# Down projection of sixteen feed-forward blocks with seven products instead of eight per pair of token tiles

## The chip, the cores and the metric

The kernel runs on one core of one Trainium2 chip. The metric is the device time of one execution in microseconds (us). The kernel before took 1143.12, 1145.43 and 1145.72 us in three runs, a median of 1145.43 us.

## The reference, cut to what matters

One layer works on 512 latent tokens and 128 context tokens of width 1024: modulation, a normalised projection, an RWKV-7 branch and a neighbourhood-attention branch, an output projection, and last a gated feed-forward network. Only the last is touched here:

```python
FF_HIDDEN = -(-8 * D_MODEL // (3 * 256)) * 256          # 2816 = 22 blocks of 128
x = x + g1 * (merged @ p["w_out"])
h2 = _rmsnorm(x, p["norm2_g"]) * (1.0 + sc2) + sh2
x = x + g2 * ((jax.nn.silu(h2 @ p["ffn_w1"]) * (h2 @ p["ffn_w3"])) @ p["ffn_w2"])
```

`g2` is a gate over the 1024 columns, one row for the latent tokens and one for the context tokens. Everything is float32.

## The kernel before, in words

The 640 tokens are five tiles of 128; tiles 0 to 3 are latent, tile 4 is context. TensorE multiplies in a rounded float32 format, so every operand is split in two: a rounded part `hi` (a cast on ScalarE) and the remainder `lo` (a subtraction on VectorE). A product is three matmuls: hi by hi, lo by hi, hi by lo. For weights, the names are `wst` (as loaded), `whi` and `wlo`.

**Up projection.** The 2816 hidden features are 22 blocks of 128. Blocks 0 and 1 are computed the plain way (`conv_gen`, beside the tail of the stage before). Each block from 2 on is computed by `pair(ft, ...)`: seven products, each of 4 x 3 matmuls of 128x128 by 128x320, into three accumulators `A_`, `B_`, `C_` (Winograd's form of Strassen's method over two halves of the width and two halves of the tokens, and the weight sums `ws` are made by `w_sum`). After each of the seven products the table `PRM["wt"]` (for block 2: `PRM["wf"]`) says which steps the other engines get next. A bare letter belongs to the block in hand, `<` to the block before it (its tail: `x h m i o`, which end in the hidden block `u` and its split), `-` to this block's own weights, `>` to the weights of the next block (`s1` to `s4` sums, `ha la hb lb` the casts of the first two of its four weight tiles).

**Down projection.** After the blocks of a part (0 to 5, 6 to 11, 12 to 17, 18 to 21; `fp=(6, 12, 18)`) `down_gen` multiplies them by their rows of `ffn_w2`, 512 columns at a time (`n` is 0 or 1): for each half, each hidden block and each of five token tiles, three matmuls of 128x128 by 128x512. `w2c(n, f)` is a tile of `ffn_w2` for the blocks f and f+1, side by side, 512 columns each. `add_gated` takes a finished accumulator, multiplies it by the gate `G` and adds it to `x2[i]`, the layer's running result; in the last part the rows are then stored.

**What sets the order.** TensorE, VectorE, ScalarE and GpSimd (POOL) work in program order here (`manual_schedule`). SyncE (SP) issues the loads; a scheduler puts them in order, and SP too works in order: a load whose buffer is not free holds back those behind it. Weight buffers come in two pools, which `weights(...)` opens. Home 0 has two buffers for `wst`, home 1 has one; each has two for `whi` and two for `wlo`. `w_stage` loads the `ffn_w1` tile ("g") of a block into home 1, and the `ffn_w3` tile ("u") into home 0. The raw tile in home 1 can be overwritten only when the last reader of the one before it is done.

Of the kernel before, what the change touches and what calls it, by code (L numbers as in the profile page):

```python
# [22 lines left out]
XB, WAB, FA = 4, 8, 2  # L23
# [35 lines left out]
     "120:W2S3A4R3W3S4X3R4X4 186:T3U3H3J3 198:T4U4H4J4 206:K0D1M0D3D2P2D4K1K2Q2V0K3N0 222:K5K7K6K8M2P3K4Q3V2N2"),  # L59
# [4 lines left out]
        ">s3 V1 N1 g >s1",  # L64
        "z >s2 >ha M3",
        "v V3 N3 >s4 >la",
        "w >hb >lb",
# [3 lines left out]
        "u -ld <i <o",  # L71
        ">s3 g >s1",
        "z >s2 >ha",
# [3 lines left out]
    fp=(6, 12, 18), h2e="dpddddpddd", x0e="a", ze="aa", y2=1, y1=0, sc=3, sr=3, sp=1, mg=1.915, h1=0.952,  # L77
# [37 lines left out]
def body(ctx: ExitStack, tc: tile.TileContext, xs, xp, cols, consts, w_ada, b_row, w_rw, w_qkv,  # L115
# [112 lines left out]
    def drain(g):  # L228
        for _ in g:
            pass  # L230
# [1505 lines left out]
    x2 = [xpool.tile([P, 1024], F32, name=f"x2_{i}") for i in range(5)]  # L1736
    G = xpool.tile([P, 2, 1024], F32, name="G")
# [5 lines left out]
    def load_gate(b):  # L1743
        ad = adr[:, :]
        for g in range(2):
            sp.dma_start(G[:, g, :], bass.AP(ad.tensor, ad.offset + g * 6144 + b * 512, [[0, P], [1, 1024]]))

    def add_gated(ps, i, n, c, a=0, b=512):
        g, sl = 0 if i < 4 else 1, slice(n * 512 + a, n * 512 + b)
        tt = sb.tile([P, 512], F32, tag="tt", bufs=2, name=nm("tt"))[:, a:b]  # L1750
        dve.scalar_tensor_tensor(out=tt, in0=ps[:, a:b], scalar=c, in1=G[:, g, sl], op0=ALU.mult, op1=ALU.mult)  # L1751
        dve.tensor_tensor(out=x2[i][:, sl], in0=x2[i][:, sl], in1=tt, op=ALU.add)
# [97 lines left out]
    steps = dict(D=t_sum, P=t_hi, Q=t_lo, M=lambda i: conv_mul(i), V=lambda i: conv_hi(i), N=lambda i: conv_lo(i), K=lambda i: first_prep(i), A=n_add, S=n_square, R=n_rstd, X=n_scale, T=lambda i: n_out(i, 0), U=lambda i: n_out(i, 1), H=lambda i: n_split(i, 0), J=lambda i: n_split(i, 1),  # L1850
# [21 lines left out]
    load_gate(10)  # L1872
    u = {}

    def hidden(ft):
        u[ft] = qp.tile([P, 2, NT], F32R, tag="q", bufs=6, name=nm("u"))
# [23 lines left out]
    def conv_a(i):  # L1900
        ca[i] = sb.tile([P, NT], F32, tag="a", bufs=2, name=nm("a"))[:, :H2]

    def conv_u(i):
        ft, n = i // 2, i % 2
        if n == 0 and ft not in u:
            hidden(ft)
        return [u[ft][:, p_, H2 * n:H2 * n + H2] for p_ in range(2)]

    def conv_mul(i):
        if i not in ca:  # L1910
            conv_a(i)
        p1, p3 = cps.pop(i)
        act.activation(ca[i], p1[:, :H2], AF.Silu)
        dve.tensor_tensor(out=ca[i], in0=ca[i], in1=p3[:, :H2], op=ALU.mult)

    def conv_hi(i):
        act.copy(conv_u(i)[0], ca[i])

    def conv_lo(i):
        hi, lo = conv_u(i)  # L1920
        dve.tensor_tensor(out=lo, in0=ca[i], in1=hi.bitcast(F32), op=ALU.subtract)
# [38 lines left out]
    def pair(ft, tag, old, now, nxt):  # L1960
# [4 lines left out]
        p1, u2, u3 = [sb.tile([P, H2], F32, tag=t, bufs=1, name=nm(t)) for t in ("p1", "u2", "u3")]  # L1965
# [10 lines left out]
        out = dict(p=lambda: act.copy(p1, A_), u=lambda: add(u2, B_, p1),  # L1976
                   g=lambda: act.activation(a[:, :H2], A_, AF.Silu),
                   z=lambda: add(u3, B_, p1), v=lambda: add(c2[:, H2:], C_, u3), w=lambda: add(c2[:, :H2], B_, p1),
                   x=lambda: add(u2, C_, u2), h=lambda: act.activation(a[:, H2:], u2, AF.Silu), m=mul, i=lambda: act.copy(u[ft][:, 0, :], a),
                   o=lambda: eng_x(PRM["oe"]).tensor_tensor(out=u[ft][:, 1, :], in0=a, in1=u[ft][:, 0, :].bitcast(F32),  # L1980
                                                            op=ALU.subtract))
        x = B2
        prods = ((A_, "a", 0, x[0, 0], True), (B_, "b", 0, BT[2], True), (A_, "a", 512, x[1, 0], False),
                 (B_, "b", 512, BT[3], False), (C_, "c", 0, BT[1], True), (B_, "d", 0, BT[4], False),
                 (C_, "c", 512, x[1, 1], False))
        for j, (ps, k, o_, x_, st) in enumerate(prods):
            for _ in mm4(ps, w[k], o_, x_, first=st, more=not st):
                pass
            for e in PRM["wf" if ft == FA else "wt"][j].split():
                if e in at1:  # L1990
                    at1[e]()
                    continue
                d = {"<": old, "-": now, ">": nxt}.get(e[0], out)
                f = d.pop(e.strip("<->"), None)
                if f:
                    f()
        return out

    at1 = {f"{k}{i}": lambda k=k, i=i: steps[k](i) for k in "PQMVN" for i in range(5)}
# [34 lines left out]

    fts = [list(range(a, b)) for a, b in zip((0,) + PRM["fp"], PRM["fp"] + (NFT,))]
    with tc.manual_schedule(engines=FIRST):
# [3 lines left out]
        for i in (1, 3):  # L2040
            conv_a(i)
        for part, fs in enumerate(fts):
            old, first, todo = {}, [], [f for f in fs if f >= FA]
            for j, ft in enumerate(todo):
                if ft < fs[-1]:
                    w_stage(ft + 1)
                    nxt = preps(ft + 1)
                else:
# [5 lines left out]
                old, now = pair(ft, ("acc", "tp")[j % 2], old, now, nxt), nxt  # L2054
            run(old, "x h m i o")
            for n in range(2):
                fin = part == len(fts) - 1 and n == 1
                pss = {}
                drain(down_gen(pss, fs, n, fin, first))
                if n == 0:  # L2060
                    first = [wload(w2c(1, f)) for f in fs[0:2 * PRM["pf"]:2]]
                elif not fin:
                    w_stage(fs[-1] + 1)
                    now = preps(fs[-1] + 1)
                    run(now, PRM["w0"])
                for i, t in pss.items():
                    down_out(i, t, n, fin, part)
# [112 lines left out]
```

## Time and profile before

| | before |
|---|---|
| median of three runs | 1145.43 us (1143.12 to 1145.72) |
| span of the profiled execution | 1142.3 us |
| what the runs show around that span | 0.8 to 3.4 us (the three times less 1142.3) |
| TensorE busy | 1108.0 us, 97% of the span |
| VectorE, ScalarE, POOL busy | 777.2, 537.9, 195.8 us |
| first block computed by `pair` starts | 741.2 us |
| one block of `pair`, steady | 12.32 us |
| one part's down projection with six blocks | 40.78 us |

The profile gives one execution: busy times of the engines, groups of instructions by line with their mean duration, what ended each wait, and the order in time. Matmuls overlap, so the pace of TensorE is read from the distance of starts and not from a duration. Times below without a unit of their own are in us from the start of the span.

### The profile page before, as it was taken

How to read it: one execution, taken by the hardware profiler on the slowest of the kernel's cores; microseconds unless marked ns; L12 is line 12 of the kernel's file. 1: busy time of each engine (PE TensorE's matmuls, PEld its weight loads, DVE VectorE, ACT ScalarE, POOL GpSimd, SP SyncE). 2: the span in 40 equal slices, each digit the busy share in tenths (PEclk: the TensorE clock that was granted, in tenths of full speed). 3: DMA queues.
4: the chain of work that ended last, by engine and by line, in shares of the span. 5: the costliest groups of instructions: out<-in, count | busy, mean ns of one | idle time of the engine just before them, and what ended most of it. 6: DMA issues, size and time to landing. Idle time of an engine off the chain costs nothing.

```text
span 1142.3 us, 26868 instructions
## 1 busy us (share of the span) xinstructions
PE 1108.0 (97%) x11160; PEld 980.2 (86%) x11160; DVE 777.2 (68%) x1641; ACT 537.9 (47%) x1060; POOL 195.8 (17%) x262
## 2 busy tenths in 40 slices
PE   5999999999999999999899999999999999999998
PEld 4688878789888988888898788999899989998997
DVE  4565465669658847945787846996478647874775
ACT  4444566665565665567343525654134413441340
POOL 1163244330101212110100511210101010101000
PEclk8999999999999999999999999999999999999999
DMA  9753677654423433344734962223212321232122
GB/s 340 262 107 102 187 268 259 200 151 112 126 64 98 130 104 94 107 108 107 266 92 126 264 214 72 78 89 112 72 56 93 111 74 56 93 106 80 56 93 93
DMA packets 60482, 149.16 MB, mean 131 GB/s; under 512 B 7460, under 2 KB 22436, under 8 KB 60360
## 3 DMA queue, kind: packets, MB, share of 16 engines
q1 hardware_dynamic: 54312, 129.85, 34.8%
q0 software_dynamic: 4032, 14.68, 6.5%
q10 hardware_dynamic: 2016, 2.90, 0.8%
q8 instruction: 88, 1.44, 0.5%
q14 instruction: 34, 0.28, 0.1%
HBM read 118.41 MB, written 14.32 MB: 116 GB/s over the span
## 4 chain that ended last, share of the span: by engine, by line
PE 76%; DVE 8%; issue 7%; ACT 4%; DMA 3%; POOL 1%; SPq 0%; ACTq 0%; DVEq 0%; POOLq 0%
PE acc L311 23%; PE f L1883 23%; PE fl L223 10%; PE mm L223 5%; DMA wa<-in_w_ada_dram 3%; PE psa L1044 1%; DVE RL L1330 1%; DVE pr L1326 1%; PE lg L959 1%; PE pt L988 1%; PE po L1006 1%; DMA win<-in_rpbp_dram 1%; PE w L1446 1%; PE fl L587 1%; PE w L1189 1%
## 5 line engine op out<-in xcount | busy, mean ns | idle before, releaser
L1883 PE MATMUL f<-t,whi 128*128 128x320 f32 x640 | 141.7, 310 | 0.2
L311 PE MATMUL acc<-whi,u 128*128 128x512 f32 (+1 forms) x448 | 136.1, 386 | 0.0
L1883 PE MATMUL f<-b,whi 128*128 128x320 f32 x608 | 135.0, 310 | 0.4 <-DVE b L212 0.4
L223 PE MATMUL fl<-h,whi 128*128 128x320 f32 x672 | 120.9, 320 | 0.0
L1883 PEld LDWEIGHTS f<-t,whi 128*128 128x128 f32 x640 | 106.8, 188 | 0.8 <-issue 0.4
L223 PEld LDWEIGHTS fl<-h,whi 128*128 128x128 f32 x672 | 101.2, 188 | 4.8 <-issue 0.2
L192 ACT CAST whi<-wst 128x1024 fp32r<-128x1024 f32 (+1 forms) x77 | 79.3, 1033 | 53.4 <-PE acc L311 41.6
L1883 PEld LDWEIGHTS f<-b,whi 128*128 128x128 f32 x608 | 101.8, 188 | 1.1 <-issue 0.6
L1883 PE MATMUL f<-t,wlo 128*128 128x320 f32 x320 | 98.9, 309 | 0.0
L311 PEld LDWEIGHTS acc<-whi,u 128*128 128x128 f32 x448 | 83.5, 188 | 16.6
L1883 PE MATMUL f<-b,wlo 128*128 128x320 f32 x304 | 94.1, 309 | 0.0
L1936 ACT CAST whi<-ws 128x1024 fp32r<-128x1024 f32 x40 | 42.0, 1051 | 104.4 <-PE f L1883 45.6
L1950 POOL TENSOR_TENSOR ws<-wst 128x512 f32<-128x512 f32 x20 | 29.2, 1462 | 334.6 <-DVE wlo L1939 226.3
L311 PE MATMUL acc<-wlo,u 128*128 128x512 f32 (+1 forms) x224 | 86.3, 385 | 0.0
L311 PE MATMUL acc<-whi,h 128*128 128x512 f32 x240 | 79.2, 404 | 0.8 <-DVE h L436 0.8
L195 DVE TENSOR_TENSOR wlo<-wst,whi 128x1024 fp32r<-128x1024 f32 (+2 forms) x57 | 60.2, 1066 | 27.8 <-ACT whi L192 27.2
L1751 DVE SCALAR_TENSOR_TENSOR tt<-acc,G 128x512 f32<-128x512 f32 (+1 forms) x51 | 34.7, 680 | 59.6 <-PE acc L311 44.7
L223 PE MATMUL fl<-h,wlo 128*128 128x320 f32 x336 | 62.7, 318 | 0.0
L1936 ACT CAST whi<-wst 128x1024 fp32r<-128x1024 f32 (+1 forms) x48 | 41.3, 869 | 42.3 <-PE acc L311 37.6
L1883 PEld LDWEIGHTS f<-t,wlo 128*128 128x128 f32 x320 | 60.1, 188 | 0.0
L1939 DVE TENSOR_TENSOR wlo<-ws,whi 128x1024 fp32r<-128x1024 f32 x40 | 55.5, 1387 | 5.4 <-ACT whi L1936 5.4
L191 POOL DMA_DIRECT2D wlo<-wst x28 | 24.8, 886 | 191.4 <-ACT wlo L190 169.9
(341 smaller groups left out, 2534.0 us busy)
## 6 DMA issues: line engine op xcount, KB each, us to landing
wst<-in_w_dram SPq DMA_DIRECT2D x66, 512.0 KB
wst<-in_w_rw_dram SPq DMA_DIRECT2D x31, 512.0 KB
wlo<-wst POOLq DMA_DIRECT2D x28, 512.0 KB, 4.7
wa<-in_w_ada_dram SPq DMA_DIRECT2D x24, 512.0 KB
f<-in_w_ada_dram SPq DMA_DIRECT2D x16, 512.0 KB
wst<-in_w_qkv_dram SPq DMA_DIRECT2D x12, 512.0 KB
o<-o_d SPq DMA_DIRECT2D x14, 320.0 KB
x<-in_xs_dram SPq DMA_DIRECT2D x8, 512.0 KB
```

The source lines that it names most:

```text
L191: pool.dma_start(lo[:, :n].bitcast(F32), st[:, :n], accum_op=ALU.add)
L192: act.copy(hi[:, :n], st[:, :n])
L195: dve.tensor_tensor(out=lo[:, a:b], in0=st[:, a:b], in1=hi[:, a:b].bitcast(F32), op=ALU.subtract)
L223: pe.matmul(ps[:, :t1 - t0], w[:, a:a + 128], x[:, k0 + kt, t0:t1], start=n == 0, stop=n == 3 * nk - 1)
L311: pe.matmul(pss[i][:, a:b], lhs(x, kt, ts_), w[:, cs_], start=ki == 0 and n == 0, stop=ki == last and n == 2)
L587: pe.matmul(ps[hf][:, :H2], u[:, kt * 128:kt * 128 + 128], x[:, kt, a:b], start=kt == 0 and n == 0, stop=kt == 7 and n == 2)
L959: pe.matmul(psl[:, hd, o_:o_ + n], qT[ft][rows, qs], x[rows, :], start=True, stop=True)
L1751: dve.scalar_tensor_tensor(out=tt, in0=ps[:, a:b], scalar=c, in1=G[:, g, sl], op0=ALU.mult, op1=ALU.mult)
L1883: pe.matmul(ps[:, :H2], w_[:, c_], x_[:, kt, :], start=first and kt + n == 0, stop=last and kt == 3 and n == 2, skip_group_check=more)
L1936: act.copy(r[0][:, :width], src())
L1939: dve.tensor_tensor(out=r[1][:, :width], in0=src(), in1=r[0][:, :width].bitcast(F32), op=ALU.subtract)
L1950: eng_x(PRM["se"][i - 1]).tensor_tensor(out=o_, in0=x, in1=y, op=op)
```

## The change

The hidden blocks 0 to 15 (`SF = 16`) are now projected down in four parts of four blocks; blocks 16 to 21 are the last part and use the old way. For a part of four blocks there are two pairs of hidden blocks (even e, odd o). For a pair, two token tiles (0 and 1, or 2 and 3) and the two column halves, the eight products are replaced by seven of Winograd's form; tile 4 keeps its eight-fold form. The products need sums of the hidden blocks (`u_steps`: raw sums in the buffer of the constants `K`, split into `SS`) and sums of the weights: four weight tiles per pair (`1` to `4`) in place of two. `1` and `2` are tiles of `ffn_w2` as they are; `3` and `4` are made by DMAs issued from POOL that add to what lies in the buffer (`acc`, used in `a3 b3 a4 b4`). The `lo` parts of `2` and `3` are made by ScalarE (minus the tile) and an adding DMA; those of `1` and `4` on VectorE.

Finished accumulators are no longer gated and added to `x`. They are added to `Y` (five tiles) and `Z` (two), which take the place of `x2` and `tt`; `x2` is stored to DRAM (`x2d`) before. At the last part, `fold` adds `Z` to `Y` by DMA, multiplies `Y` by the gate and adds `x2d` by DMA, in the blocks 16 to 19. The gate's second load moves to that place. `PRM["sd"]` says which steps the other engines get after each of the 17 groups of matmuls (`DOWN`); `l30` is the `lo` of tile 3 of pair 0, `h30` its `hi`, `z y b c d e f q` the evictions, `>` the next block's weights as above.

```diff
-XB, WAB, FA = 4, 8, 2
+XB, WAB, FA, SF = 4, 8, 2, 16
     wf=(
         "P1 p Q1 -hc -hd -lc",
         "u -ld P4 Q4 M1",
-        ">s3 V1 N1 g >s1",
+        ">s3 i0 t0 o0 >s1",
         "z >s2 >ha M3",
-        "v V3 N3 >s4 >la",
-        "w >hb >lb",
+        "v t1 i1 >s4 >la",
+        "w g o1 >hb j1 >lb k1",
         ""),
     wt=(
         "<x -hc <h p -hd -lc <m",
-        "u -ld <i <o",
-        ">s3 g >s1",
-        "z >s2 >ha",
+        "u -ld <i <t <o",
+        ">s3 g >s1 <j",
+        "z >s2 >ha <k",
         "v >s4 >la",
         "w >hb >lb",
         ""),
-    fp=(6, 12, 18), ...
+    sd=("l31 <x <h l30 <m", "z0 <i <t", "z1 <o <j", "<k h31 h30", "", "q0", "y0 y1 h40 h41", "l40 b0", "b1 l41", "",
+        "c0 c1 l20 h20 l21 h21", "d0", "d1", ">s3 >s1 >s2 >s4", "e0 e1 >ha >la", "", ">hb >lb", "f0 f1 q1"),
+    fp=(4, 8, 12, 16), ...
+    def u_steps(ft, a):
...
+        def e_hi():
+            act.copy(sv(ft, 0, 4), two(a))
+            act.copy(raw_s(0), two(a[:, 128:]))
+            act.copy(EP[p][:, 0, :], a[:, 512:640])
+        def e_lo():
+            low(sv(ft, 1, 4), two(a), sv(ft, 0, 4))
+            low(EP[p][:, 1, :], a[:, 512:640], EP[p][:, 0, :])
+        def e_sum():
+            dve.tensor_tensor(out=raw_s(2), in0=two(a), in1=two(a[:, 128:]), op=ALU.subtract)
+        def o_sum():
+            s1, s2_, s3, s4 = [raw_s(j) for j in range(4)]
+            dve.scalar_tensor_tensor(out=s2_, in0=s3, scalar=-1.0, in1=two(a[:, 128:]), op0=ALU.mult,
+                                     op1=ALU.subtract)
+            dve.tensor_tensor(out=s4, in0=two(a), in1=s2_, op=ALU.add)
+            dve.tensor_tensor(out=s1, in0=s1, in1=two(a[:, 128:]), op=ALU.subtract)
...
+        return dict(t=o_sum, i=lambda: act.copy(u[ft][:, 0, :], a), o=lambda: low(u[ft][:, 1, :], a, u[ft][:, 0, :]),
+                    j=lambda: act.copy(sh(), K[:, 0:1024]), k=lambda: low(sl(), K[:, 0:1024], sh()))
...
+    def acc(dst, src):
+        pool.dma_start(dst, src, accum_op=ALU.add)
...
+            def lo():
+                alloc()
+                if dma:
+                    act.activation(r[1], wd[0], AF.Copy, scale=-1.0)
+                    pool.dma_start(r[1].bitcast(F32), wd[0], accum_op=ALU.add)
+                else:
+                    dve.tensor_tensor(out=r[1], in0=wd[0], in1=r[0].bitcast(F32), op=ALU.subtract)
...
+        def load(k):
+            for p, f in enumerate(pr):
+                cast(k, p, wdma(w2c(int(k) - 1, f), 1 - p), k == "2")
...
+        def a3():
+            for p, f in enumerate(pr):
+                w = w2c(0, f)
+                acc(V(raw[3, p][:, :], [[512, 2], [1, 512]]), V(w, [[0, 2], [1, 512]]))
+        def b3():
+            for p, f in enumerate(pr):
+                acc(raw[3, p][:, 512:1024], w2c(1, f)[:, 0:512])
...
+        def ev(k, i, n, op):
+            sl = Y[i][:, n * 512:n * 512 + 512] if i is not None else Z[n]
+            dve.tensor_tensor(out=sl, in0=sl, in1=ps(k), op=op)
...
+        for g, names in zip(DOWN, PRM["sd"][1:]):
+            for terms, items in g:
+                for xh, wh in terms:
+                    for it in items:
+                        b, k, half, kind, tp, p = it
+                        pe.matmul(ps(b), lhs(kind, xh, fs, p, tp), U[k][p][wh][:, half * 512:half * 512 + 512],
+                                  start=b not in started, stop=True, skip_group_check=True)
+                        started.add(b)
+            hooks(names)
+    p3 = pr_("C", "2", 1, "4")
+    DOWN = ([(F_, pr_("A", "1", 0, "a", (0,)))], [(F_, pr_("A", "1", 0, "a", (1,)))], [(F_, q0[:3])],
+            [(F_, pr_("A", "1", 1, "b", ps_=(0,)))], [(F_, q0[3:]), (F_, pr_("A", "1", 1, "b", (0,), (1,)))],
+            [(F_, pr_("A", "1", 1, "b", (1,), (1,)))],
+            [(F_, pr_("B", "3", 1, "2", (0,)))], [(F_, pr_("B", "3", 1, "2", (1,)))],
+            [(F_, pr_("C", "3", 0, "1", ps_=(0,)))], [(F_, pr_("C", "3", 0, "1", ps_=(1,)))],
+            [(F_, pr_("B", "4", 1, "3", (0,)))], [(F_, pr_("B", "4", 1, "3", (1,)))],
+            [(F_, pr_("B", "4", 0, "d", ps_=(0,)))], [(F_, pr_("B", "4", 0, "d", ps_=(1,)))],
+            [(H, p3)], [(H, q1)], [(L, p3), (L, q1)])
...
+                if sf and j == len(todo) - 2:
+                    D_["load3"]()
+                    for k, n in ((2, "a3"), (6, "b3")):
+                        ext.setdefault(k, []).append(D_[n])
+                elif sf and j == len(todo) - 1:
+                    ext.setdefault(1, []).insert(0, D_["load4"])
+                    for k, n in ((3, "a4"), (5, "b4")):
+                        ext.setdefault(k, []).append(D_[n])
+                old, now = pair(ft, ("acc", "tp")[j % 2], old, now, nxt, ext), nxt
+            if sf:
+                D_["load"]("2")
+                w_stage(fs[-1] + 1)
+                now = preps(fs[-1] + 1)
+                down_strassen(fs, U, T, old, now)
+                if part == len(fts) - 2:
+                    exts = fold()
+                continue
```

The order in which SP issues loads, at the passage from the first down projection to the next part. Before (hidden blocks 0 to 5; `wst_10833` is the g tile of the next block, 6, in home 1; `wst_10835` its u tile; `wst_10797` the last tile of `ffn_w2`):

```order
L174 DMA wst_10705<-in_w_dram 128x1024 [waits DMAHW6_49,DVE_49]
L174 DMA wst_10835<-in_w_dram 128x1024 [waits DMAHW7_49,DVE_49]
L174 DMA wst_10797<-in_w_dram 128x1024 [waits DMAHW1_49,DVE_49]
L174 DMA wst_10868<-in_w_dram 128x1024 [waits DMAHW0_49,DVE_49]
L174 DMA wst_10833<-in_w_dram 128x1024 [waits DMAHW3_49,DVE_49]
```

After (blocks 0 to 3; `wst_10388` is the g tile of the next block, 4, `wst_10390` its u tile; `wst_10384` and `wst_10386` are tile 2 of pair 0 and 1; `t_1443`, `t_1442` belong to tile 3 of the part after):

```order
L176 DMA wst_10386<-in_w_dram 128x1024 [waits DVE_49,Pool_49]
L176 DMA wst_10384<-in_w_dram 128x1024 [waits DMAHW1_49,DVE_49]
L176 DMA wst_10390<-in_w_dram 128x1024 [waits DMAHW7_49,DMAHW6_49,DVE_49]
L2118 DMA t_1443_10841<-in_w_dram 128x1024 [waits DMASW5_49,DMASW4_49,DMASW7_49,DMASW3_49,Activation_49]
L2118 DMA t_1442_10839<-in_w_dram 128x1024 [waits DMASW6_49,DMASW5_49,DMAHW0_49,DMASW2_49,Activation_49]
L176 DMA wst_10388<-in_w_dram 128x1024 [waits DMAHW5_49,DMASW6_49,Activation_49]
L176 DMA wst_10579<-in_w_dram 128x1024 [waits DMAHW2_49,DMAHW4_49,DMASW7_49,Activation_49]
```

The g tile's load waited for VectorE; now it waits for a DMA issued from POOL (`DMASW6`, the adding DMA of `l20`) and for ScalarE (`h20`), the two readers of tile 2 of pair 0, which lies in the one raw buffer of home 1.

VectorE at the same passage. Before (from the last `lo` of `ffn_w2` on; the sums of block 6, its first two casts, and then the evictions of the half n = 1):

```order
L195 TENSOR_TENSOR wlo_10800<-wst_10797,whi_10799 128x1024 [waits DMAHW3_49,Activation_49]
L1950 TENSOR_TENSOR ws_10837<-wst_10833,wst_10835 128x512 [waits DMAHW5_49,DMAHW2_49]
L1950 TENSOR_TENSOR ws_10837<-wst_10835,ws_10837 128x512 [waits DVE_49]
L1950 TENSOR_TENSOR ws_10838<-wst_10833,ws_10837 128x512 [waits DVE_49]
L1939 TENSOR_TENSOR wlo_10844<-wst_10833,whi_10843 128x1024 [waits PE_49,Activation_49]
L1939 TENSOR_TENSOR wlo_10848<-ws_10837,whi_10847 128x1024 [waits Activation_49]
L1751 SCALAR_TENSOR_TENSOR tt_10851<-acc_10732,G 128x512 [waits PE_49]
```

After (from the last eviction `d1` on; the sums of block 4, the evictions `e0 e1`, the casts `la lb`, then `f0 f1`):

```order
L2170 TENSOR_TENSOR Y_10078<-Y_10078,y_10472 128x512 [waits DVE_49,PE_49]
L1989 TENSOR_TENSOR ws_10527<-wst_10388,wst_10390 128x512 [waits DMAHW6_49,DMAHW1_49]
L1989 TENSOR_TENSOR ws_10527<-wst_10390,ws_10527 128x512 [waits DVE_49]
L1989 TENSOR_TENSOR ws_10528<-wst_10388,ws_10527 128x512 [waits DVE_49]
L2170 TENSOR_TENSOR Y_10076<-Y_10076,y_10463 128x512 [waits PE_49]
L2170 TENSOR_TENSOR Y_10078<-Y_10078,y_10472 128x512 [waits PE_49]
L1978 TENSOR_TENSOR wlo_10542<-wst_10388,whi_10541 128x1024 [waits Activation_49]
L1978 TENSOR_TENSOR wlo_10563<-ws_10527,whi_10562 128x1024 [waits Activation_49]
L2170 TENSOR_TENSOR Y_10075<-Y_10075,y_10481 128x512 [waits PE_49]
L2170 TENSOR_TENSOR Y_10077<-Y_10077,y_10483 128x512 [waits PE_49]
```

In both orders the first sum of the next block waits for its g and u tile; now two evictions stand between the sums and the first cast, and three more behind the second.

More of the change, by code (lines that the diff above doesn't have):

```diff
@@ L1898, in body, with conv_a, conv_mul @@
     ca = {}
-    def conv_a(i):
-        ca[i] = sb.tile([P, NT], F32, tag="a", bufs=2, name=nm("a"))[:, :H2]
-    def conv_u(i):
+    def conv_a(ft):
+        ca[ft] = sb.tile([P, NT], F32, tag="a", bufs=2, name=nm("a"))
+    def conv_mul(i):
         ft, n = i // 2, i % 2
-        if n == 0 and ft not in u:
-            hidden(ft)
[L1907 to L1921, printed above, removed]
+        if ft not in ca:
+            conv_a(ft)
+        c = ca[ft][:, H2 * n:H2 * n + H2]
+        p1, p3 = cps.pop(i)
+        act.activation(c, p1[:, :H2], AF.Silu)
+        dve.tensor_tensor(out=c, in0=c, in1=p3[:, :H2], op=ALU.mult)
+        if n:
+            hidden(ft)
+            at1.update((f"{k}{ft}", f) for k, f in u_steps(ft, ca[ft]).items())
     W = {}
```

169 lines of the change are left out of this document (141 added, 28 removed).

## Prediction

> **What bounds the kernel now.** I read the page first: busy times, the slices and the chain.
>
> ```profile
> PE 1108.0 (97%) x11160; PEld 980.2 (86%) x11160; DVE 777.2 (68%) x1641; ACT 537.9 (47%) x1060; POOL 195.8 (17%) x262
> PE   5999999999999999999899999999999999999998
> PE 76%; DVE 8%; issue 7%; ACT 4%; DMA 3%; POOL 1%; SPq 0%; ACTq 0%; DVEq 0%; POOLq 0%
> ```
>
> TensorE is busy in nearly every slice, and the last 14 of the 40 (the feed-forward network) are full. Then the stage itself, in stretches of one block of `pair` and of one down projection with six blocks; a row is the stretch, its length, busy PE, PEld, DVE, ACT, POOL with their instructions, the granted clock, the share of the DMA engines and GB/s.
>
> ```profile
> 869.19:881.51 12.32, 12.32 (x86) 12.32 (x86) 10.19 (x15) 5.52 (x8) 1.30 (x1) 1.00 0.25 85
> 906.15:946.93 40.78, 40.78 (x181) 33.76 (x181) 23.11 (x31) 7.39 (x8) 3.21 (x2) 1.00 0.25 86
> ```
>
> TensorE has no hole in either, at a granted clock of 1.00. VectorE has 2.1 us to spare in a block. So a matmul less is its time less, as long as nothing makes TensorE wait. The pace comes from the starts:
>
> ```profile
> 909.99 0.39 PE L311 MATMUL acc<-wlo,u 128*128 128x512 f32 x1
> 946.71 0.39 PE L311 MATMUL acc<-wlo,u 128*128 128x512 f32 x1
> 946.94 0.45 PE L1883 MATMUL f<-b,whi 128*128 128x320 f32 x2
> 947.23 0.31 PE L1883 MATMUL f<-b,wlo 128*128 128x320 f32 x1
> ```
>
> Between the first two starts lie 54 products of three matmuls: 36.72 / 54 = 0.680 us each, 0.2267 a matmul. A block begins with two matmuls on `whi` (0.29 us); the third needs `wlo`.
>
> **What the change removes.** In `DOWN` I count 36 products for four blocks; the old way has 4 x 2 x 5 = 40. Four parts save 16 products: 16 x 0.680 = 10.9 us. Every other matmul stays, so this is all there is to gain.
>
> **What it adds at each passage to the next part.** I count time t from the end of a part's last product of `pair`. The 36 products take 24.48 us. The passage before:
>
> ```profile
> 920.87 0.39 PE L311 MATMUL acc<-wlo,u 128*128 128x512 f32 x1
> 921.30 0.69 DVE L1751 SCALAR_TENSOR_TENSOR tt<-acc,G 128x512 f32<-128x512 f32 x1 [6.07 <-PE acc L311]
> 922.02 0.69 DVE L1752 TENSOR_TENSOR x<-x,tt 128x512 f32<-128x512 f32 x1
> 922.66 0.69 DVE L1751 SCALAR_TENSOR_TENSOR tt<-acc,G 128x512 f32<-128x512 f32 x1
> ...
> 928.07 1.22 DVE L195 TENSOR_TENSOR wlo<-wst,whi 128x1024 fp32r<-128x1024 f32 x1
> 932.87 0.69 DVE L1950 TENSOR_TENSOR ws<-wst,wst 128x512 f32<-128x512 f32 x1 [3.58 <-DMA wst<-in_w_dram]
> 933.60 1.42 DVE L1950 TENSOR_TENSOR ws<-wst,ws 128x512 f32<-128x512 f32 x2
> 934.94 1.22 DVE L1939 TENSOR_TENSOR wlo<-wst,whi 128x1024 fp32r<-128x1024 f32 x1
> ```
>
> ```profile
> 929.32 0.33 SPq L174 DMA_DIRECT2D wst<-in_w_dram  x1
> ```
>
> VectorE's `lo` ends at 929.29, SP issues the next block's g tile 0.03 later, and the first weight sum starts 3.55 us after that. From there 2.07 us of sums, then the first `lo`. It is done at 936.16, and the block begins at 946.94: 10.8 us of cover.
>
> After the change that cover is gone. The g tile goes into home 1, whose one raw buffer holds tile 2 of pair 0 until `l20` has read it, and `l20` is now ScalarE plus an adding DMA. What that costs, from the kernel's other casts of this kind:
>
> ```profile
> 664.67 1.06 ACT L190 ACTIVATE wlo<-wst 128x1024 fp32r<-128x1024 f32 x1 [1.17 <-PE acc L311]
> 666.03 0.87 POOL L191 DMA_DIRECT2D wlo<-wst  x1 [3.56 <-ACT wlo L190]
> ```
>
> ```profile
> L191 POOL DMA_DIRECT2D wlo<-wst x28: 852/872/1050, 245.2 to 666.0; - x28
> DMA to landing us min/median/max: 4.4/4.7/7.4
> ```
>
> Step by step. `l20` needs the `wlo` buffer of tile 3 of pair 0, last read by the ninth group: 18 products, t = 12.24. An eviction started 0.43 after the start of its last matmul above, so ScalarE starts at 12.24 - 0.23 + 0.43 = 12.44 and ends at 13.50. POOL starts 0.30 later (665.73 to 666.03): 13.80. It lands 4.7 later: 18.50. SP and load, 0.03 + 3.55: the g tile is there at 22.08. Sums 2.07: 24.15. Then `e0 e1`, two evictions 0.64 apart (922.02 to 922.66): 25.43. First `lo`, 1.22: 26.65. TensorE wants it at 24.48 + 0.29 = 24.77. It waits 1.9 us. With the shortest landing the wait is 1.6, with the longest 4.6; should the chain shrink by 2 us it is nothing. I take 1.9, since the median is the row nearest to a quiet stretch. Behind `la` on VectorE stand `lb` (done 1.15 later, wanted 1.76 later), `f0 f1 q1` and the third cast, wanted seven microseconds into the block: nobody else waits. There are four such passages: 4 x 1.9 = 7.6 us.
>
> The Trainium skill, "DMA: Bandwidth & Descriptors", section "Anatomy of one DMA", gives about 2.0 us plus bytes over 436 GB/s; for 512 KB that makes an estimate of 3.2 us for each of the two transfers. The wait would then be 22.08 - 1.5 - 0.35 + 4.57 - 24.77, which is nothing. The rows disagree: none of the 28 landed under 4.4.
>
> **The rest of the added work.** VectorE gets for a pair of blocks four sums of 128x256, split casts and one `lo` of 128x1024; the nearest rows:
>
> ```profile
> L1939 DVE TENSOR_TENSOR wlo<-ws,whi 128x1024 fp32r<-128x1024 f32 x40 | 55.5, 1387 | 5.4 <-ACT whi L1936 5.4
> L212 DVE TENSOR_TENSOR b<-hq,b 128x256 fp32r<-128x256 f32 x4 | 1.7, 425 | 1.2 <-ACT b L211 1.1
> ```
>
> In the block that carries an odd tail this is 3 x 0.43 + 1.39 = 2.7 us on 10.19, or 12.9 for 12.32: 0.6 too much, once a part, and the block behind it has neither sums nor third and fourth casts to prepare. A block's second `lo` has slack:
>
> ```profile
> 868.38 1.22 DVE L1939 TENSOR_TENSOR wlo<-ws,whi 128x1024 fp32r<-128x1024 f32 x1
> ```
>
> It ends at 869.60 and is wanted at 869.19 + 1.76 + 0.29 = 871.24. So 0.6 costs nothing. Without that cover: 0.6 x 3.
>
> The first block of `pair` is already short of VectorE:
>
> ```profile
> 753.19 1.22 DVE L1939 TENSOR_TENSOR wlo<-wst,whi 128x1024 fp32r<-128x1024 f32 x1
> 754.48 0.39 PE L1883 MATMUL f<-b,wlo 128*128 128x320 f32 x1
> 756.26 2.14 DVE L1939 TENSOR_TENSOR wlo<-ws,whi 128x1024 fp32r<-128x1024 f32 x1
> ```
>
> The `lo` ends at 754.41 and TensorE's first `wlo` matmul follows at 754.48: no slack. Ahead of it come now the sums `t0`, `t1` (4 x 0.43) and the two parts of `o0` (0.43 and less), about 2.4, and two casts of 0.49 leave; the second `lo` also gets `o1` (0.82) ahead of it. Two more casts of that kind leave the stretch before. I take 1.5 us of waiting, bounds 0 and 3. POOL clears `Y` and `Z` beside it: a clearing of 128x1280 took 1.49 us, seven smaller ones fit beside 1.30 busy in a block, though VectorE's 2.14 against 1.39 shows what a POOL instruction beside it can do; hence the upper bound.
>
> ```profile
> L1639 POOL MEMSET Nt<- 128x1280 f32 x1 | 1.5, 1490 | 0.0
> ```
>
> `fold` puts ten multiplications of 0.69 (as the gating above) into two blocks: 10.19 + 3.45 = 13.64 for 12.32, 2.6 too much in two blocks, 1.64 covered by the slack: 0 to 1.0, I take 0.5. The adding DMAs on POOL (12 a part at 0.87 is 10.5 us of its 73.8) come in order, and `b3` waits for `a3`; they start in the third block and tile 3 is wanted 33 us later, so they are hidden; without cover a landing, 4.7. Stores of `x`, loads of the gate and the last adds of `x2d` end blocks ahead of their readers: nothing.
>
> **Sum.** -10.9 + 7.6 + 1.5 + 0.5 = -1.3 us. The profiled execution's span is 1142.3, so 1141.0; the median of the runs stands 3.1 above that span, and 1144.1 is the forecast. Bounds of the likely case: four waits of 1.6 and no other cost, -4.5; four of 2.6 and 4.0 of other costs, +3.5: 1140.9 to 1148.9.
>
> **Rivals.**
>
> *The tile is there in time.* If landing and load together are 2 us shorter, or the two transfers ahead overlap more than the rows show, the passages cost nothing: -10.9 + 2.0 = -8.9, 1136.5. For it: the 4.7 is taken beside other traffic, and this stage moves only a share of 0.25. Against: even the shortest landing leaves 1.6. The fit of the Trainium skill cited above gives this case too.
>
> *The adding DMAs land late.* They do so in traffic:
>
> ```profile
> 638.00:667.00 29.00, 27.61 (x133) 21.27 (x132) 21.72 (x39) 16.90 (x27) 20.59 (x21) 1.00 0.94 272
> DMA to landing us min/median/max: 5.5/6.2/7.2
> ```
>
> With 0.94 of the DMA engines in use, five landings took 5.5 to 7.2. A part now moves some 13 MB in 73.8 us (16 weight tiles, 8 adds of 256 or 512 KB, 4 casts of 512 KB), an estimate of 176 GB/s against 85, and `l21` runs beside the g tile. A landing of 7.2 makes a wait of 4.4: -10.9 + 17.6 + 2.0 = +8.7, 1154. From a landing of 5.1 the passages eat the whole gain; from 5.9 it is slower. Against: the bulk of the traffic falls in the blocks, not between t = 13.8 and 18.5.
>
> *VectorE is the bound.* If POOL's issues stretch VectorE as in the 2.14 us row (0.75 more), each of the three blocks with odd tails costs 1.4 and the first 3.0: -10.9 + 7.6 + 4.2 + 3.0 + 1.0 = +4.9, 1150.3.
>
> **How the numbers follow.** What can be told from no change is 0.3%, 3.4 us: 1142.0 to 1148.9. I give the forecast 0.58, the tile in time 0.20, late landings 0.13, VectorE 0.09. Of the forecast, whose bounds run from -4.5 to +3.5, I put 0.14 below -3.4, 0.42 within, 0.02 above. So faster 0.34, same 0.48 (0.42, and 0.06 of the rivals that stop short), slower 0.18. The range reaches into both sides: 1137 to 1151.
>
> **What would show it.** Right: TensorE's rows show four holes of 1 to 3 us, each 0.29 us into a part's first block, with VectorE's first `lo` ending just ahead and its sums released by the g tile's load, SP's load by the adding DMA on `wlo`. The down projection of four blocks takes 24.5 us. Wrong: no hole there (the tile came in time), holes inside the 24.5 us (tile 3 or the hidden sums late, which I hold to be covered), or blocks of `pair` longer than 12.32 beyond the first. If the parts' down projections come out over 24.5 without holes, the count or the pace is wrong.

## The result and the profile after

The changed kernel takes 1156.0 us (median of 4 runs, 1153.7 to 1157.3) against 1144.3 for the kernel before (median of 4): a ratio of 1.0099, 95% interval 1.0078 to 1.0120. It is slower by 11.7 us; forecast was no change, with 1151 as the upper end. The profiled execution has a span of 1154.1 us, 11.8 above the one before.

The page of the changed kernel: busy times, TensorE's slices, and the two DMA queues that matter (packets, MB, share of the 16 engines' time; q1 carries the plain loads and stores, q0 what POOL issues, all of it adding DMAs).

```profile
PE 1102.5 (96%) x11118; PEld 971.1 (84%) x11118; DVE 801.2 (69%) x1701; ACT 578.7 (50%) x1114; POOL 253.3 (22%) x326
PE   6999999999999999999899999999999989989998
q1 hardware_dynamic: 58488, 140.86, 37.1%
q0 software_dynamic: 13520, 37.75, 17.8%
```

Matmuls were saved, yet two more slices of the last third are no longer full (the very last one was not full before either). The stretches show where (same columns as in the prediction; cut at TensorE's starts: the four down projections, the blocks between the first and the second, those behind the fourth, one block by itself).

```profile
766.70:794.06 27.36, 25.26 (x110) 20.13 (x109) 16.72 (x26) 13.35 (x15) 4.51 (x5) 1.00 0.78 196
844.80:874.77 29.97, 26.89 (x110) 21.27 (x109) 16.73 (x26) 13.36 (x15) 4.52 (x5) 0.94 0.76 188
925.48:953.99 28.51, 25.25 (x110) 20.13 (x109) 16.68 (x26) 13.31 (x15) 4.51 (x5) 1.00 0.77 194
1004.76:1032.85 28.09, 25.27 (x110) 20.12 (x109) 16.61 (x26) 13.24 (x15) 4.51 (x5) 1.00 0.79 201
...
794.06:844.80 50.74, 49.55 (x338) 49.28 (x336) 42.57 (x64) 23.17 (x36) 11.76 (x12) 1.00 0.57 149
1032.85:1108.87 76.02, 74.53 (x505) 73.92 (x504) 68.16 (x94) 31.79 (x46) 16.24 (x14) 1.00 0.58 141
878.50:890.80 12.30, 12.30 (x86) 12.30 (x85) 9.76 (x15) 4.70 (x8) 1.70 (x2) 1.00 0.31 108
```

A block of `pair` keeps its 12.3 us. A down projection of four blocks was to take 24.48; it takes 27.36 to 29.97, in all 113.93, which is 16.0 too much. The blocks between (4 x 12.32 = 49.28) take 1.46 more, the last six (73.92) 2.10 more. The waits of TensorE from 700 us on (us in total, times, longest):

```profile
PE y L2191 <- DMA wlo<-t: 9.0, 4, 2.7
PE f L1930 <- DVE wlo L1978: 5.1, 5, 1.3
PE y L2191 <- DVE Y L2170: 2.2, 4, 0.6
PE f L1930 <- ACT p L2015: 0.6, 1, 0.6
PE f L1930 <- ACT whi L1975: 0.5, 1, 0.5
```

The largest, 9.0, is not at a passage. It lies inside the down projection, and what ends it is an adding DMA into the `lo` of tile 3. The second part on TensorE, in order of time:

```profile
856.66 0.73 PE L2191 MATMUL y<-wlo,ss 128*128 128x512 f32 x2 [2.52 <-DMA wlo<-t]
...
866.62 0.97 PE L2191 MATMUL y<-whi,u 128*128 128x512 f32 x3 [0.56 <-DVE Y L2170]
...
876.40 0.41 PE L1930 MATMUL f<-b,wlo 128*128 128x320 f32 x1 [1.17 <-DVE wlo L1978]
```

These are the three kinds of wait that every part has: for the `lo` of tile 3, for an eviction (`d1`, on accumulator B1), and at the passage, which alone was forecast. ScalarE, POOL and SP ahead of the first of them:

```profile
843.24 1.06 ACT L2101 ACTIVATE wlo<-t 128x1024 fp32r<-128x1024 f32 x1 [2.62 <-PE f L1930]
845.52 0.47 ACT L2018 ACTIVATE a<-u 128x320 f32<-128x320 f32 x1 [1.22 <-DVE u L2010]
845.90 1.04 ACT L2101 ACTIVATE wlo<-t 128x1024 fp32r<-128x1024 f32 x1
```

```profile
840.99 2.10 POOL L2078 DMA_DIRECT2D t<-t  x2
844.59 0.86 POOL L2102 DMA_DIRECT2D wlo<-t  x1 [1.50 <-ACT wlo L2101]
847.24 0.86 POOL L2102 DMA_DIRECT2D wlo<-t  x1 [1.79 <-ACT wlo L2101]
```

```profile
843.13 2.09 SPq L176 DMA_DIRECT2D wst<-in_w_dram  x2
```

ScalarE's part of `l31` waits for TensorE; that of `l30` stands behind a step of the tail (`x`), which waits for VectorE. `l30` is sent at 847.24 and TensorE wants it 9.07 after the start of the stage (40 matmuls), at 853.87. A landing of 4.7 would have been in time by 1.9 us. TensorE starts again at 856.66, 9.4 us after the issue. The landings of this kind over the whole kernel (bytes in KB, median us), with `b4` as the third row:

```profile
wlo<-wst POOLq DMA_DIRECT2D x36, 512.0 KB, 4.8
wlo<-t POOLq DMA_DIRECT2D x8, 512.0 KB, 9.3
t<-t POOLq DMA_DIRECT2D x8, 256.0 KB, 7.2
```

The 36 are the casts of the earlier stages and of tile 2. The eight of tile 3 take twice as long. In the 12.07 us from the issue of `l31` to the end of the wait, the DMA engines are full (share 1.00):

```profile
844.59:856.66 12.07, 9.55 (x44) 7.54 (x42) 8.93 (x14) 7.04 (x8) 1.71 (x2) 1.00 1.00 233
```

### The profile page after: what moved, and what is told of

It is laid out like the page before. It is cut to its first block, busy times and chain, and to the rows that moved or that the text cites. A ratio compares the mean times of both kernels' runs of the same rounds, so it can differ in the third digit from the quotient of the medians.

```text
span 1154.1 us, 27120 instructions
## 1 busy us (share of the span) xinstructions
PE 1102.5 (96%) x11118; PEld 971.1 (84%) x11118; DVE 801.2 (69%) x1701; ACT 578.7 (50%) x1114; POOL 253.3 (22%) x326
## 3 DMA queue, kind: packets, MB, share of 16 engines
q1 hardware_dynamic: 58488, 140.86, 37.1%
q0 software_dynamic: 13520, 37.75, 17.8%
## 5 line engine op out<-in xcount | busy, mean ns | idle before, releaser
L194 ACT CAST whi<-wst 128x1024 fp32r<-128x1024 f32 (+1 forms) x67 | 68.9, 1030 | 39.0 <-PE acc L313 27.1
L193 POOL DMA_DIRECT2D wlo<-wst x28 | 24.8, 887 | 192.4 <-ACT wlo L192 176.2
L197 DVE TENSOR_TENSOR wlo<-wst,whi 128x1024 fp32r<-128x1024 f32 (+2 forms) x47 | 48.1, 1032 | 26.1 <-ACT whi L194 25.9
L1930 PEld LDWEIGHTS f<-b,wlo 128*128 128x128 f32 x304 | 57.1, 188 | 6.3 <-DVE wlo L1978 6.3
L1473 DVE TENSOR_TENSOR ZV<-w,Dt 64x128 f32<-64x128 f32 x64 | 18.5, 289 | 54.5 <-PE w L1461 53.4
L313 PEld LDWEIGHTS acc<-whi,h 128*128 128x128 f32 x240 | 45.2, 191 | 12.6 <-issue 2.4
L225 PEld LDWEIGHTS fl<-h,wlo 128*128 128x128 f32 x336 | 51.2, 188 | 1.9
L2170 DVE TENSOR_TENSOR Y<-Y,y 128x512 f32<-128x512 f32 x56 | 36.9, 684 | 22.7 <-PE y L2191 22.7
```

The source lines that it names most:

```text
L193: pool.dma_start(lo[:, :n].bitcast(F32), st[:, :n], accum_op=ALU.add)
L194: act.copy(hi[:, :n], st[:, :n])
L197: dve.tensor_tensor(out=lo[:, a:b], in0=st[:, a:b], in1=hi[:, a:b].bitcast(F32), op=ALU.subtract)
L225: pe.matmul(ps[:, :t1 - t0], w[:, a:a + 128], x[:, k0 + kt, t0:t1], start=n == 0, stop=n == 3 * nk - 1)
L313: pe.matmul(pss[i][:, a:b], lhs(x, kt, ts_), w[:, cs_], start=ki == 0 and n == 0, stop=ki == last and n == 2)
L1473: dve.tensor_tensor(out=V(ZV[own, l + 1, h, :], [[128 * dl, 2], [1, 64]]), in0=V(pn[own, :], [[64, 2], [1, 64]], 64 * g), in1=V(Dt[own, 0, ...
```

## The experiments

Each is an edit of the changed kernel; ratios are to the kernel before, in the same batch of runs, with 95% intervals. The stages ahead of the feed-forward network, which no edit touches, end anywhere from 721.5 to 727.0 in these profiles, so the times of a few runs can differ by 2 to 3 us for a reason that lies ahead of the edits. The stretch from TensorE's start of the first down projection to the last matmul's start leaves that out, but it is read from one profiled execution of each kernel. Both are listed, in the order of the text.

| | time (us) | ratio | stretch (us) |
|---|---|---|---|
| the changed kernel | 1156.0 | 1.0099 | 383.1 |
| three loads later | 1146.2 | 1.0038 | 371.7 |
| `b4` on VectorE | 1150.7 | 1.0079 | 374.5 |
| lo of tile 3 on VectorE | 1145.5 | 1.0022 | 371.2 |
| lo of tile 2 on VectorE | 1153.0 | 1.0104 | 376.5 |
| accumulator by accumulator | 1159.7 | 1.0149 | 382.4 |
| late loads and this order | 1152.9 | 1.0085 | 377.1 |
| all three edits | 1140.1 | 0.9973 | 365.7 |
| `l20` behind `d0` | 1136.4 | 0.9951 | 363.1 |
| the first block too | 1137.2 | 0.9947 | 363.0 |

### Why the lo of tile 3 lands late

**Three loads later.** A load waits until one column of its buffer has been written by VectorE, which happens behind the step `k`, after the fourth group.

```diff
-    ... "<k h31 h30", "", "q0", ...
+    ... "<k h31 h30", "w2", "q0", ...
     def wdma(src, home=None, touch=False):
         st = pl.tile([P, 1024], F32, tag="wst", bufs=nst, name=nm("wst"))
+        if touch:
+            dve.memset(st[:, 0:1], 0.0)
...
-                D_["load"]("2")
-                w_stage(fs[-1] + 1)
...
+                def tile2():
+                    D_["load"]("2")
+                    W[fs[-1] + 1] = dict(g=wdma(w13[2 * fs[-1] + 2], 1), u=wdma(w13[2 * fs[-1] + 3], 0, True))
+                    now.update(preps(fs[-1] + 1))
+                T["w2"] = tile2
```

`touch` is set for both tiles 2 and for the next block's u tile (`load` passes it on for tile 2).

> The loads of tile 2 (two of 512 KB) and of the next block's u tile (512 KB) start after the fourth group instead of 1 to 7 us ahead of the first. Theory of full engines: the lo of tile 3 lands late because loads and adding DMAs share the DMA engines (share 0.99 in the first 12 us); with up to 1.5 MB less in that stretch its landing falls from 8.4 to 9.7 us to about 6, the holes inside the down projections (1.8 to 3.0 us each) go, about -9: 1147. Theory of POOL's queue: the landing is set by the adding DMAs ahead of it in POOL's queue alone; the holes stay within 0.7 us, 1154 to 1157. Theory of its own price: an adding DMA from such a tile takes 8 to 9 us whatever runs beside it; the holes stay, 1156.

Ratio 1.0038 (1.0019 to 1.0056); the stretch is 11.4 shorter. Second part and the blocks behind it, and the landings of the eight:

```profile
846.66:872.18 25.52, 24.96 (x110) 20.21 (x109) 16.74 (x29) 13.44 (x15) 4.52 (x5) 1.00 0.88 238
872.18:922.83 50.65, 49.55 (x337) 49.28 (x336) 42.38 (x64) 23.09 (x36) 11.79 (x12) 1.00 0.56 145
```

```profile
wlo<-t POOLq DMA_DIRECT2D x8, 512.0 KB, 4.8
```

The landing falls from 9.3 to 4.8, the row of waits for it is gone, and each down projection takes 25.5. Nothing in POOL's queue was changed, so neither that queue alone nor a price of this kind of transfer explains the 9.3. A full share by itself does not explain it either: while the two DMAs are under way here, with no load of SP beside them, the share is as high as in the changed kernel.

```profile
846.46:852.50 6.04, 6.04 (x29) 4.97 (x28) 5.33 (x10) 4.11 (x6) 1.71 (x2) 1.00 1.04 199
```

What differs is how much other work the engines have at that time.

**b4 on VectorE.**

```diff
-                acc(raw[4, p][:, 0:512], raw[3, p][:, 512:1024])
+                dve.tensor_tensor(out=raw[4, p][:, 0:512], in0=raw[4, p][:, 0:512], in1=raw[3, p][:, 512:1024], op=ALU.add)
```

> The step b4 (raw tile 4 plus half of raw tile 3, two adding DMAs of 256 KB between buffers of the core, issued 3.5 us ahead of the lo of tile 3) becomes two additions of 128x512 on VectorE. Theory of POOL's queue: the lo of tile 3 no longer stands behind them, lands 2 to 4 us sooner, the holes go nearly all: -7 to -10, 1146 to 1149. Theory of full engines: 0.5 MB less in traffic of about 237 GB/s is 2 us sooner: -6 to -8, 1148 to 1150. Theory of its own price: no change, 1156. VectorE gets 1.4 us more in the last block of a part, which it has to spare; a loss of up to 0.5 a part if not.

Ratio 1.0079 (1.0060 to 1.0098), which cannot be told from the changed kernel's; the stretch is 8.6 shorter. The loads are early again, the two adding DMAs ahead are gone:

```profile
PE y L2191 <- DMA wlo<-t: 1.3, 2, 0.7
```

```profile
wlo<-t POOLq DMA_DIRECT2D x8, 512.0 KB, 7.2
```

Of 9.0 us of waiting 1.3 are left. So either neighbour taken away shortens the landing, the one in POOL's queue to 7.2, those in SP's to 4.8: what is shared is the DMA engines (that it is they, and not the memory behind them, rests on the share of 1.00 and was not tested apart). The theory of the queue alone, which gave the loads no part, falls with the run before; the theory of a price of its own falls with both.

**lo of tile 3 on VectorE**, which takes away the two landings themselves. The table also moves the casts `h31 h30` to the front and the eviction `q0` back to behind the ninth group, so more than the expectation says is changed.

```diff
-    sd=("l31 <x <h l30 <m", "z0 <i <t", "z1 <o <j", "<k h31 h30", "", "q0", "y0 y1 h40 h41", "l40 b0", "b1 l41", "",
+    sd=("h31 <x <h h30 <m", "z0 <i <t", "z1 <o <j", "<k", "l30 l31", "", "y0 y1 h40 h41", "l40 b0", "b1 l41", "q0",
-                cast("3", p, home(p, t), True)
+                cast("3", p, home(p, t), False)
```

> The lo of tile 3 is made by VectorE (two of 1.22 us, after the split of the odd block's sums) in place of ScalarE and an adding DMA; nothing else changes, the loads start early as in the changed kernel. Theory (the landing of these two adding DMAs is what TensorE waits for): the holes of 1.8 to 3.0 us inside the down projections go, -9 to -11, 1146. Rival: VectorE has 8.3 us of work in the 8.2 us between the split and the second lo of tile 4, so that lo is late, and 0.5 to 1.5 of hole stay in each part: 1149 to 1152.

Ratio 1.0022 (1.0012 to 1.0033). The down projections take 25.5, as with late loads:

```profile
842.50:868.01 25.51, 24.95 (x111) 20.19 (x109) 18.47 (x28) 11.58 (x13) 3.01 (x3) 1.00 0.65 175
```

VectorE was not late, with `q0` out of its way; the rival falls.

### The passage and the eviction

**lo of tile 2 on VectorE.**

```diff
-        "c0 c1 l20 h20 l21 h21", "d0", "d1", ...
+        "c0 c1 h20 l20 h21", "d0", "d1 l21", ...
-                cast(k, p, wdma(w2c(int(k) - 1, f), 1 - p), k == "2")
+                cast(k, p, wdma(w2c(int(k) - 1, f), 1 - p), False)
```

> The lo of tile 2 is made by VectorE (1.22 us each) in place of ScalarE and an adding DMA; so the next block's g tile can be loaded some 4 us sooner. Theory: the waits of 1.35 us (with the slower matmul behind, 1.46) at the start of a part's first block come from the adding DMA of l20 ahead of that load; all four go, 4 x 1.46 = 5.8: 1150.2. Rival: VectorE, with 2.4 us more in the last third of the down projection, becomes late with d0, d1 or the weight sums; then a wait of about 1 us takes their place and the time stays within 2 us of 1156.

Ratio 1.0104 (1.0080 to 1.0127), by which it cannot be told from the changed kernel; the stretch is 6.6 shorter. The blocks behind a down projection have no wait left, and the last six keep 0.55.

```profile
796.30:845.59 49.29, 49.29 (x338) 49.28 (x336) 39.36 (x61) 22.54 (x35) 11.42 (x12) 1.00 0.56 152
1029.30:1103.77 74.47, 74.27 (x506) 73.92 (x505) 63.92 (x91) 30.96 (x45) 14.88 (x13) 1.00 0.56 141
```

So the passage's wait came from the adding DMA ahead of the g tile, as the prediction's chain has it. The 0.55 lie at one place in the third of the six blocks, where TensorE waits for a step of VectorE behind a multiplication by the gate: so it is `fold`, whose multiplications these are.

**Accumulator by accumulator.** B1 is finished by the twelfth group, and the second matmul of the thirteenth writes it again, 0.23 later, while `d1` (0.69) still reads it.

```diff
-            [(F_, pr_("B", "4", 0, "d", ps_=(0,)))], [(F_, pr_("B", "4", 0, "d", ps_=(1,)))],
+            [(F_, pr_("B", "4", 0, "d", (0,)))], [(F_, pr_("B", "4", 0, "d", (1,)))],
```

> Only the order of two groups of the down projection changes: the product of tile 4 with the odd block's columns is done first for accumulator B0 with both pairs, then for B1 (before: B0 and B1 alternating, so that B1 is written one matmul after its group ended, while its eviction d1, 0.69 us, runs). Theory: the hole ahead of the second matmul of that group (0.83 us of TensorE's starts in each of four parts) is this eviction, so 4 x 0.83 = 3.3 us go: 1152.7 against 1156.0. Rival: VectorE is late there anyway because of the late lo of tile 3; then the wait moves to the next group and less than 1 us goes.

Ratio 1.0149 (1.0109 to 1.0189): no gain, against the expectation, and 0.7 in the stretch. The eviction's wait is gone, as expected, but it came back:

```profile
848.06:875.15 27.09, 24.97 (x111) 20.20 (x110) 16.00 (x25) 12.64 (x14) 4.54 (x5) 1.00 0.82 206
875.15:926.59 51.44, 49.54 (x337) 49.27 (x336) 43.17 (x65) 23.88 (x37) 11.78 (x12) 1.00 0.57 149
```

```profile
PE f L1930 <- DVE wlo L1978: 8.0, 5, 2.0
```

The blocks behind take 51.4 instead of 50.7. So less than 1 us goes, as the rival has it, but the wait moved to the passage and not to the next group: the chain over the g tile starts from the ninth group, so a wait behind that group had hidden part of it. What TensorE no longer waits for `d1` it waits for `la`.

**Both, late loads and this order**, to test that reading where no other wait is left.

> The loads of tile 2 and of the u tile late, and the product of tile 4 with the odd block accumulator by accumulator; the lo of tile 2 still by an adding DMA. Theory: the hole of 0.83 in the down projection goes, but the next block's first lo is set by the chain from the ninth group (lo of tile 2, its landing, the g tile, its sums) and not by TensorE's end, so the wait at the passage grows by the same 0.83: the stretch from the first down projection on is as with the late loads alone (371.7), 1146. Rival: the chain itself starts from a group that moves up, then 3.3 less, 1143.

Ratio 1.0085 (1.0065 to 1.0105): worse than the late loads alone, by 5.4 in the stretch, where no change was expected. The blocks behind the first part, then the second part's down projection and the blocks behind it; the last row is a piece of these.

```profile
793.24:844.66 51.42, 49.54 (x337) 49.27 (x336) 43.25 (x65) 23.86 (x37) 11.75 (x12) 1.00 0.53 139
844.66:869.33 24.67, 24.67 (x111) 20.29 (x109) 15.22 (x26) 12.00 (x13) 4.54 (x5) 1.00 0.92 246
869.33:923.06 53.73, 51.07 (x337) 50.81 (x336) 43.99 (x66) 24.52 (x37) 11.77 (x12) 0.97 0.53 134
871.80:876.20 4.40, 3.76 (x15) 3.76 (x16) 4.40 (x6) 0.86 (x2) 1.27 (x1) 0.61 0.36 119
```

The down projection is at its 24.67 without a hole. Behind the first part the reading holds: 51.42 against 50.72 with the late loads alone, so 0.70 of the 0.83 is handed on. Behind the second the passage takes 4.45 instead of 1.37. The landings of tile 2 are 5.5 and 6.1 there (4.4 and 5.4 in this part with the late loads alone; why they differ was not settled), and behind the wait TensorE's granted clock is 0.61 over some 4 us. The third and the fourth passage have such a slow stretch too, at some 1.5 us each. In all the four down projections take 3.4 less than with the late loads alone and the blocks behind them 8.7 more, of which the slow stretches are about 4.6.

### Together

**All three edits** (late loads, the order of the accumulators, the lo of tile 2 on VectorE).

> Three edits together: the loads of tile 2 and of the u tile start after the fourth group, the product of tile 4 with the odd block goes accumulator by accumulator, and the lo of tile 2 is made by VectorE. Theory: every wait that the change brought into the down projections and the passages goes; from the first down projection to the last matmul four times 24.6, three times 49.3, 74.5 and 41.0, together 361.7 against 383.1 of the changed kernel: 21.4 less, 1134.6, some 8 us under the kernel before. Rival: VectorE, with 2.4 us more in the last third and less time to do it in, becomes late with d0, d1 or lo of tile 4; 0.5 to 1.5 a part stay, 1137 to 1140.

Ratio 0.9973 (0.9961 to 0.9984). The rival came: in the second part TensorE still loses 0.6 us to an eviction, and VectorE's rows show what stands ahead of it (`l20`, then `d0` and `d1`).

```profile
843.69:869.12 25.43, 24.95 (x110) 20.20 (x109) 21.77 (x34) 12.31 (x13) 2.79 (x3) 1.00 0.67 196
```

```profile
858.57 1.53 DVE L2106 TENSOR_TENSOR wlo<-wst,whi 128x1024 fp32r<-128x1024 f32 x1
860.02 1.27 DVE L2172 TENSOR_TENSOR Y<-Y,y 128x512 f32<-128x512 f32 x2
```

**l20 behind d0**, shown against the run with all three edits.

```diff
-        "c0 c1 h20 l20 h21", "d0", "d1 l21", ">s3 >s1 >s2 >s4", "e0 e1 >ha >la", ...
+        "c0 c1 h20 h21", "d0 l20", "d1 l21", ">s3 >s1 >s2 >s4", "e0 >ha >la e1", ...
```

> As the run with all three edits, but VectorE makes the lo of tile 2 of pair 0 behind the eviction d0 instead of ahead of it, and the last eviction e1 goes behind the next block's first lo. Theory: the 0.6 to 1.2 us that TensorE waits there for d0 in each part come from that lo ahead of it on VectorE; they go, the down projections take 24.7 each, and the stretch from the first down projection to the last matmul is 362.6 against 365.7: 3 us less, 1137. Rival: the chain over the g tile's load, 0.7 us later now, reaches the first block of a part; then a wait of 0.2 to 0.7 appears there and the time stays at 1138.5 to 1140.

1136.4 us against 1142.9 for the kernel before, ratio 0.9951 (0.9934 to 0.9969): faster, by 6.4 us. The down projections take 24.8, but for the third with 25.2; the second and the blocks behind it:

```profile
844.52:869.28 24.76, 24.76 (x111) 20.22 (x109) 20.42 (x33) 12.32 (x13) 2.81 (x3) 1.00 0.66 200
869.28:918.56 49.28, 49.28 (x337) 49.28 (x336) 40.89 (x63) 22.52 (x35) 11.76 (x12) 1.00 0.57 149
```

**The first block**, shown against the run before.

```diff
-        "w g o1 >hb j1 >lb k1",
+        "w g >hb j1 >lb o1",
...
-        exts = [..., {0: [lambda: [pool.memset(t, 0.0) for t in Y[3:] + Z]]}]
+        exts = [..., {0: [lambda: [pool.memset(t, 0.0) for t in Y[3:] + Z], lambda: at1.pop("k1")()]}]
```

> As the run before, and in the first block of the up projection that is made by seven products VectorE gets o1 behind the casts and k1 only in the block after. Theory: the waits that this block has beyond the kernel before (1.6 us) come from these two instructions ahead of a second lo and of the steps of the next block; about 1.2 of them go: 1136. Rival: VectorE is full through both blocks (11.5 us busy in 12.3), so the wait comes back a block later: no change to 1137.

Ratio 0.9947 (0.9928 to 0.9967), not to be told from the run before. The edit lies ahead of the stretch of the table; from TensorE's first matmul of the up projection to the first down projection it is 58.15 against 58.46, a gain of 0.3 where 1.2 was expected. The wait of 0.6 for `p` is gone, and one came back later in the same block of TensorE, near what the rival has:

```profile
764.28 0.41 PE L1932 MATMUL f<-t,whi 128*128 128x320 f32 x1 [0.57 <-DVE u L2012]
```

## Why the prediction was wrong

**The step that failed** is the one on the adding DMAs: "they start in the third block and tile 3 is wanted 33 us later, so they are hidden; without cover a landing, 4.7". That holds for `a3` and `b3`, the sums of the raw tile: those of `a3` took 8.3 (median), and TensorE waited for none. The same tile's `lo` is made by one more adding DMA per pair. The prediction counts these among its 12 and gives them no start of their own; they start behind the last products of `pair` and its tail, around the start of the down projection (844.59 and 847.24 against 844.80). The cover of the second was 1.9 us over a quiet landing, not 33. The landing was 9.3, and four waits with 9.0 us came of it. This is the sign of being wrong that the prediction itself names, "holes inside the 24.5 us (tile 3 or the hidden sums late, which I hold to be covered)". With their restarts the four waits are about 10 us of the 16.0; `d1`, a wait that the prediction does not contain, is 3.3 (0.83 of TensorE's starts a part), one slow stretch of TensorE in the second part about 1.6, and the rest some 0.25 a part, which remains in the best run (24.76 against 24.48).

The other steps, one by one:

- *What bounds, and the removal, -10.9:* right, but for 0.2 to 0.3 a part. Where no wait is left a down projection takes 24.67 to 24.76, against 40.8 x 4/6 = 27.2 before: 2.5 a part, 10 in all.
- *The passage, 4 x 1.9:* the mechanism was right, and each link shows in the rows below (second part: the adding DMA of `l20`, the first sum, `e0 e1`, the first `lo`). The landing is 4.4 (4.7 was taken), and SP's load is there 4.3 after its issue (3.55 was taken): two misses that cancel in part, which is luck. In the changed kernel the wait is 1.2 (1.46 with its restart, 5.9 in all against 7.6), because the eviction's wait behind the ninth group hid 0.8 of it. Without that cover, with the accumulators in order, it is 1.9 to 2.0; 1.9 was worked out.

```profile
863.12 0.86 POOL L2102 DMA_DIRECT2D wlo<-wst  x1 [15.03 <-ACT wlo L2101]
871.87 0.69 DVE L1989 TENSOR_TENSOR ws<-wst,wst 128x512 f32<-128x512 f32 x1 [5.30 <-DMA wst<-in_w_dram]
873.93 1.28 DVE L2170 TENSOR_TENSOR Y<-Y,y 128x512 f32<-128x512 f32 x2
875.13 1.22 DVE L1978 TENSOR_TENSOR wlo<-wst,whi 128x1024 fp32r<-128x1024 f32 x1
```

- *The first block, 1.5:* right in size, and VectorE is the cause. The loss lies in the block behind the first, whose `lo` the first prepares (14.09 against 12.54 before, by TensorE's starts): a few tenths of waiting for `wlo`, and 0.6 for `p`, which stands on ScalarE behind a step that waits 3.2 for VectorE (the last experiment moves steps of VectorE alone, and that wait is gone). The first block itself is 13.03 against 12.98, though it holds the wait of 0.5 for `whi`.
- *fold, 0.5:* 0.55.
- *VectorE in the odd tails, hidden:* right; blocks take 12.3. The 2.14 us that the prediction holds up as what a POOL instruction can do stood in the kernel before beside an addition of weight sums on POOL (756.02, 1.30 us), not beside a DMA issue; beside the issue at 847.24 VectorE's steps keep their 0.42.
- *The landing of 4.4 to 7.4 as one price for all adding DMAs:* too narrow. It held for tile 2 (4.4 and 5.3 in the second part), not for the `lo` of tile 3 (9.3), and not for `a3` (8.3), which was hidden.

So -10.9 + 1.5 + 5.9 + 0.5 + 16.0 makes +13.0. The spans differ by 11.8, and the stages ahead end 1.6 earlier in the later profile (TensorE's first full row of the network starts at 721.95 against 723.57), which makes 13.4; 0.4 stays open.

The rival of late landings came near with 1154 and is the right mechanism at another place; that its number is near is luck, since it puts 17.6 us on the passages, which cost 5.9. It saw that a part moves twice the bytes, and laid the delay on `l20`, against which it then noted that "the bulk of the traffic falls in the blocks, not between t = 13.8 and 18.5". That was so. It did not ask which adding DMA stands where the traffic is. The share of the engines could have been estimated too: before, q0 moved 14.68 MB in 6.5% of 16 engines' time, q1 129.85 in 34.8%, so that a megabyte by an adding DMA takes 1.65 times the engines' time.

The Trainium skill, "DMA: Bandwidth & Descriptors", section "SWDGE vs HWDGE vs iDMA", says that the two kinds of queue feed the same engines, which take turns between them. That they feed the same engines, the runs agree with: three loads of SP moved away halve the landing of POOL's DMAs, 9.3 to 4.8. The taking of turns itself no run here shows.

## What to carry to other kernels

A transfer's cover is the time from when it *can* start to when it is wanted, taken for each transfer by itself; the first steps of the same tile say nothing of its last. Price it with the traffic that runs at that moment on all queues, since DMAs of different queues share the engines. And a wait that is removed pays only if no other chain ends just behind it: fix the chain that ends last first, or the gain moves to the next wait.

## What the runs showed of the hardware

**A wait can cost TensorE twice.** Behind the wait of 2.52 us in the second part the matmuls of 512 start 0.427 apart instead of 0.227, for eight of them (3.4 us), and the granted clock of that stretch is 0.66, which is what 3.4 of 5.0 us at half the clock come to:

```profile
859.16 1.91 PE L2191 MATMUL y<-whi,ss 128*128 128x512 f32 x4
```

```profile
857.00:862.00 5.00, 5.00 (x16) 3.96 (x15) 2.51 (x3) 0.23 (x1) 0.00 (x0) 0.66 0.41 124
```

Each such stretch costs some 1.5 to 1.7 us. In the profiles of the changed kernel and of three experiments (the order of the accumulators, the lo of tile 2 on VectorE, and the late loads with the order) 13 waits of 2.0 to 2.9 us stand, and 6 have it behind them: those of 2.02, 2.08, 2.45, 2.52, 2.66 and 2.86, while 2.70 and 2.92 have not. No wait under 2.0 in these profiles has it. The Trainium skill, "TensorE: Matmul & The Clock Gate", section "Part 1: The HAM clock gate (the "warmup" mystery)", has the clock drop to half after an idle window of about 3.4 us, with a window that runs free of the kernel. The half agrees with the 0.66; that it strikes one wait and spares a longer one fits the free window; that 2.02 us are enough does not fit the length, and the measurement decides.

**An adding DMA is dear to the engines.** In the changed kernel 37.75 MB in q0, all of adding DMAs, took 17.8% of their time and 140.86 MB in q1, plain loads and stores, 37.1%: per megabyte 1.8 times as much. Whether the adding costs it or the queue is not shown, since no run moves plain bytes through q0.
